# Up to layer 0's first scores: the adaLN scale into 128 columns, gates in program order, V's weights split beside them, an order by hand for K, Q and V

## The chip, the cores and the metric

One Trainium2 chip, one of its cores. The time is the device time of one launch in microseconds (us). For the kernel before the median of three runs is given, and one further execution was recorded by the hardware profiler; the rows quoted come from that one. Engines go by the profile's names: PE (TensorE), DVE (VectorE), ACT (ScalarE), POOL (GpSimd) and SP, whose queue issues most transfers.

## What is computed

Two layers over 1024 latent tokens and 256 context tokens of 1024 features. Layer 0 is multi-head latent attention with 16 heads. All that the change touches lies in layer 0, up to the first scores:

```python
m = jax.nn.silu(cvec) @ w + b            # adaLN: shift, scale, gate of each sample
shift, scale, gate = jnp.split(m, 3, axis=-1)
h = x * (1.0 + scale[:, None, :]) + shift[:, None, :]
h_c = ctx * (1.0 + scale_c) + shift_c
q_lat, kv_lat, k_pe, gate = jnp.split(t @ w_in, splits, axis=-1)   # 256, 128, 32 and 1024 columns
q = (rms_norm(q_lat, g_qa) @ w_qb).reshape(bsz, n, A_HEADS, A_NOPE + A_ROPE)
kv = (rms_norm(kv_lat, g_kva) @ w_kvb).reshape(bsz, n, A_HEADS, A_NOPE + A_V)
```

Then come rotary terms on the 32-column parts, attention over all 1280 keys, o times silu(gate), a product with out_w and a layer norm. The context's modulation vector is c_ctx, the latents' is c.

## The kernel before

Tokens lie in ten tiles of 128: 0 to 7 are latents, 8 and 9 the context. A float32 product is three products of a high and a low half (`mm3`, L184 to L187): high by high, low by high, high by low; a split is a rounded copy on ACT (L176) and a subtraction (L177) on DVE or POOL.

**Start (L205 to L264).** The eight row blocks of adaLN's scale weights (`g` = 1) and shift weights (`g` = 0) arrive in a ring of six buffers `adaw`. For the scale PE forms two rows of 1024 (one for each sample, products L229 of 512 columns); they are copied out by ACT, turned into columns by eight small transposes (`rows_to_cols`, L192) and copied to `cols0` by DVE. For the shift DVE sums the weights into `hacc` (L233), and PE reduces over the partitions by eight products with one column of ones (L243), first for sample 1 (context), then for sample 0; DVE copies these (L244). Then `h_part` scales and shifts x: ACT the high half hH (L254), DVE the full value (L255), DVE or, for every third block, POOL the low half hL (L257). Context comes first, then tokens 0 to 511, then the rest beside the latent tiles.

**Latents (L338 to L368).** For tiles 8, 9, 0, 1 and on, PE makes 416 columns of latents (24 products), ACT and POOL the norms, DVE `ln` (L363); two tiles later `lat_post` turns ln (L331) and splits it into latH and latL. Then the first two gate tiles follow.

**Gates (L310, L520 to L546).** Four blocks of 256 gate columns by ten tiles, 24 products each, into bank tags a and d; ACT applies silu and stores. Beside each gate tile two steps of the generator `side` run: `up_weights` (weights of Q and K scaled on DVE, split on ACT and POOL; rotary part of K; squares on ACT L425 to L429 whose column sums PE takes, L414; scale factors) and `ada_dve` (three thirds of adaLN's weights summed over the blocks on DVE, L467 and L469; PE reduces over the partitions, L476, or for the last third L488). Behind them `ab1_of` and `h1_range` (L505 to L518) make the factors of layer 1. In this stage the order on every engine is the scheduler's; ahead of it, in the latents, and after it PE follows the program (`manual_schedule`).

**K, Q, V (L573 to L826).** V's weights are loaded, scaled by DVE (L291) and split; then K's first pair of heads, Q's rotary part with its rotation, Q's first heads and V's ten tiles, each product into one of three pairs of banks `a`, which ACT empties (high half, L181 or L592) and then DVE (low half, L182 or L598; for odd V tiles ACT L595 and POOL L596). `max0` (L682) takes each row's largest score: four products and reductions (L695), a last one for the context keys (L700), and a product that puts the bound into Q (L704, L705). The first scores of attention are L769.

**Attention.** `run_step` (L736) interleaves the scores' units of one head with side work for the next ones, in program order on PE.

## Time and profile before

| what | us |
|---|---|
| median of three runs (lowest to highest) | 1840.31 (1835.49 to 1841.04) |
| the profiled execution's own time | 1831.31 |
| its span | 1829.5 |
| PE busy in the span | 1680.2 (92%) |
| DVE, ACT, POOL busy | 1238.1, 1104.9, 812.0 |
| first gate product at | 96.12 |
| gates until | 240.3 |
| first scores (L769) at | 276.34 |

A row of the windows gives a stretch of the span, its length, the busy time of each engine with its number of instructions, the clock that PE was granted (1.00 is full), the share of time that the transfer engines were busy and what they moved. A row of the timeline gives start, length, engine, line, operation, what it writes and reads, and in brackets how long the engine was idle ahead of it and what ended that. A group's row gives a count, busy time, mean of one in ns and idle time ahead. PE's records overlap: a product's record is longer than its distance to the next.

### The profile page before, as it was taken

To read this page: it belongs to the slowest core of one execution; us is meant where nothing else is said; L and a number is where in the kernel's file an instruction comes from. 1 tells how busy PE (TensorE), PEld (TensorE's weight loads), DVE (VectorE), ACT (ScalarE), POOL (GpSimd) and SP (SyncE) were. 2 spreads that over 40 slices of the span, in tenths; PEclk is the share of its full clock that TensorE was granted. 3 is DMA by queue.
4 is the path that set the end of the run, shared out by engine and by line. 5 is a ranking of instruction groups with operands and counts; after the bars stand their busy time and mean duration, and the time that the engine had idled before them with its cause. 6 is when DMAs were issued, how large, how long until landed. Compare 5 with 4: busy or idle time off the path is not lost. (4 is left out here: it accounts for less than half of the span.)

```text
span 1829.5 us, 36574 instructions
## 1 busy us (share of the span) xinstructions
PE 1680.2 (92%) x14468; PEld 1229.2 (67%) x14468; DVE 1238.1 (68%) x2054; ACT 1104.9 (60%) x2223; POOL 812.0 (44%) x719
## 2 busy tenths in 40 slices
PE   7899989999999998979999999999899999886998
PEld 3889965666666655567766666767575767575776
DVE  7546765565565666636754877787777787879674
ACT  3442157877877777825435576757676676757442
POOL 1443026767767776737551323231313131435454
PEclk9999999999999999999999999999999999999999
DMA  8246630111110122164432213121212122223331
GB/s 305 71 127 191 192 109 18 40 33 37 40 45 23 40 56 68 55 211 150 142 109 76 77 53 78 53 74 52 60 41 63 44 58 62 66 60 110 100 124 70
DMA packets 111225, 154.84 MB, mean 85 GB/s; under 512 B 13415, under 2 KB 84679, under 8 KB 111054
## 3 DMA queue, kind: packets, MB, share of 16 engines
q1 hardware_dynamic: 102654, 144.90, 26.7%
q10 hardware_dynamic: 8400, 7.61, 1.3%
q8 instruction: 114, 1.87, 0.4%
q14 instruction: 57, 0.47, 0.1%
HBM read 98.65 MB, written 27.07 MB: 69 GB/s over the span
## 5 line engine op out<-in xcount | busy, mean ns | idle before, releaser
L715 POOL TENSOR_TENSOR pl<-p,ph 128x1024 f16<-128x1024 f32 (+1 forms) x176 | 364.2, 2075 | 148.0 <-ACT ph L714 121.6
L1259 ACT ACTIVATE p<-ps_b,mx 128x512 f32<-128x512 f32 (+1 forms) x384 | 230.7, 618 | 85.5 <-DVE mx L1255 81.3
L713 ACT ACTIVATE p<-ps_a,esc 128x1024 f32<-128x1024 f32 (+1 forms) x176 | 189.2, 1075 | 94.4 <-PE ps_a L771 86.9
L695 DVE TENSOR_REDUCE mx<-ps_a 128x1 f32<-128x1024 f32 x128 | 155.5, 1222 | 134.0 <-PE ps_a L693 134.0
L714 ACT CAST ph<-p 128x1024 f16<-128x1024 f32 (+1 forms) x176 | 177.1, 1006 | 5.5
L1253 DVE TENSOR_REDUCE mx<-ps_b 128x1 f32<-128x512 f32 x256 | 165.3, 679 | 0.0
L784 PE MATMUL ps_d<-Vh,pl 128*128 128x65 f16 x1344 | 145.9, 194 | 3.9 <-POOL pl L715 3.9
L781 PE MATMUL ps_d<-Vh,ph 128*128 128x65 f16 x1344 | 148.0, 195 | 0.0
L783 PE MATMUL ps_d<-Vl,ph 128*128 128x64 f16 x1344 | 146.8, 193 | 0.0
L1236 PE MATMUL ps_b<-KS,QS 128*128 128x512 f16 (+1 forms) x384 | 126.9, 347 | 12.7 <-DVE pl L182 6.9
L1284 POOL TENSOR_TENSOR sm<-sm,us 128x1 f32<-128x1 f32 x64 | 17.1, 267 | 272.2 <-DVE sm L1263 268.7
L781 PEld LDWEIGHTS <-ph 128*128 128x128 f16 x1344 | 123.2, 97 | 18.0 <-issue 4.8
L783 PEld LDWEIGHTS <-ph 128*128 128x128 f16 x1344 | 123.9, 98 | 12.0
L1237 PE MATMUL ps_b<-KS,Q 128*128 128x512 f16 (+1 forms) x384 | 129.8, 347 | 0.0
L769 PE MATMUL ps_a<-qH,KH 100*128 100x512 f16 x320 | 122.0, 381 | 7.7 <-ACT p L713 3.8
L784 PEld LDWEIGHTS <-pl 128*128 128x128 f16 x1344 | 123.1, 97 | 5.3 <-POOL pl L715 5.3
L1272 PE MATMUL ps_b<-idr,p 128*128 128x128 f32 x640 | 103.1, 277 | 25.4 <-ACT p L1259 16.8
L182 DVE SCALAR_TENSOR_TENSOR pl<-ps_b,lcf,ph 128x512 f16<-128x512 f32 (+1 forms) x192 | 117.2, 653 | 13.4 <-ACT ph L181 13.4
L181 ACT ACTIVATE ph<-ps_b,lcf 128x512 f16<-128x512 f32 (+1 forms) x192 | 115.3, 648 | 17.8 <-PE ps_b L1272 17.8
L770 PE MATMUL ps_a<-qH,KL 96*128 96x512 f16 x320 | 121.8, 381 | 0.0
L771 PE MATMUL ps_a<-qL,KH 96*128 96x512 f16 x320 | 121.2, 379 | 0.0
L1282 PE MATMUL ps_b<-vh,pl 128*128 128x128 f16 x640 | 111.3, 220 | 5.3 <-DVE pl L182 5.3
(412 smaller groups left out, 5270.3 us busy)
## 6 DMA issues: line engine op xcount, KB each, us to landing
ws<-in_dw SPq DMA_DIRECT2D x28, 512.0 KB, 3.9
adw<-in_ada_w SPq DMA_DIRECT2D x24, 512.0 KB, 4.6
adaw<-in_ada_w SPq DMA_DIRECT2D x16, 512.0 KB, 5.9
g<-sg_d SPq DMA_DIRECT2D x16, 512.0 KB, 3.6
sg_d<-gg ACTq DMA_DIRECT2D x40, 128.0 KB, 2.9
o_d<-op SPq DMA_DIRECT2D x7, 640.0 KB, 3.7
xt<-in_xT SPq DMA_DIRECT2D x16, 256.0 KB, 3.5
wgs<-in_w_in SPq DMA_DIRECT2D x32, 128.0 KB, 2.3
```

Source lines behind the costliest of these rows:

```text
L695: dve.tensor_reduce(mx[:, t, 0:1], ps, axis=AX.X, op=ALU.max)
L713: act.activation(p32[:, :n], st, AF.Exp, scale=esc0)
L714: act.copy(ph[:, :n], p32[:, :n])
L715: pool.tensor_tensor(pl[:, :n], p32[:, :n], ph[:, :n], op=ALU.subtract)
L769: pe.matmul(s_, kh[:nr, ks], QH[:nr, :], start=True, stop=False)
L781: pe.matmul(pv[:, t, :], ph[:, ts], Vh[:, k, h, :], start=(k == kcs[0] and t == 0), stop=False, skip_group_check=True)
L783: pe.matmul(pv[:, t, :V0], ph[:, ts], Vl[:, k, h, :], start=False, stop=False, skip_group_check=True)
L784: pe.matmul(pv[:, t, :], pl[:, ts], Vh[:, k, h, :], start=False, stop=(k == NT - 1), skip_group_check=True)
L1236: pe.matmul(out, qs[m][:, ts], ks[m][:, c0:c0 + n], start=True, stop=False)
L1237: pe.matmul(out, q1[m][:, ts], ks[m][:, c0:c0 + n], start=False, stop=True)
L1253: dve.tensor_reduce(mx[:, 2 + 2 * m + i:3 + 2 * m + i], b, axis=AX.X, op=ALU.max, negate=True)
L1259: act.activation(p[m][:, c0:c0 + n], b, AF.Exp, bias=nb, accum_out=sm[:, 2 + 3 * m + i:3 + 3 * m + i])
```

## The change

- **Scale.** POOL copies silu(c) to 128 columns (`scb`, the two samples in turn); PE multiplies each 128-column piece of the weights by it, so that the sums stand in PSUM as columns; two DVE additions bring them to `cols0`. The row with adaLN's bias takes one of the six `adaw` slots. PE follows the program from here until K, Q and V.
- **Shift.** PE multiplies by all 128 columns of ones. The context's comes first; four products with an identity and the first half of tile 8 follow, then the other sample's, then the rest of tile 8.
- **Latents.** `lat_post` runs three tiles behind, with one more buffer for ss, rs and ln.
- **Gates.** One step of `side` for each gate tile. `up_weights` works in a ring of five buffers `u`, its low halves are DVE's, squares are summed one square later. `ada_dve` has three buffers acc; a third's column sums stand beside the next third's additions. V's weights are split beside the last block of gates.
- **Layer 1's range** (`h1_range`) runs within the first step of attention, in parts.
- **K, Q, V.** PE and DVE follow an order by hand: Q's rotary part first, then K, then V's first tile, Q, and on. Even V tiles go by ACT and POOL, odd ones by DVE.

The diff, cut to its core:

```diff
+    rowb = hs.tile([P, D], F32, tag="adaw", bufs=6, name="rowb")[0:1, :]
...
-    bks = [bank("a"), bank("a")]
-    for j in range(2):
-        pe.matmul(bks[j][:2, :], ones[0:1, 0:2], rowb[:, j * 512:(j + 1) * 512], start=True, stop=False)
+    man = ExitStack()
+    man.enter_context(tc.manual_schedule(engines={ENG[c] for c in MAN}))
+    cbs = [bank("c").rearrange("p (j n) -> p j n", j=4) for _ in range(2)]
+    scb = hs.tile([P, KT, P], F32, name="scb")
+    pool.tensor_copy(scb.rearrange("p k (n s) -> p k n s", s=2),
+                     sc.rearrange("p (k o s) -> p k o s", o=1, s=2).to_broadcast([P, KT, 64, 2]))
+    for j in range(KT):
+        pe.matmul(cbs[j // 4][:, j % 4, :], rowb[:, j * P:(j + 1) * P], ones[0:1, :], start=(j % 4 == 0), stop=False,
+                  skip_group_check=True)
...
             if g:
-                for j in range(2):
-                    pe.matmul(bks[j][:2, :], sc[:, 2 * k:2 * k + 2], w[:, j * 512:(j + 1) * 512],
-                              start=False, stop=(k == KT - 1))
+                for j in range(KT):
+                    pe.matmul(cbs[j // 4][:, j % 4, :], w[:, j * P:(j + 1) * P], scb[:, k, :], start=False,
+                              stop=(k == KT - 1), skip_group_check=True)
...
-    for j in range(2):
-        act.copy(rows[:, j * 512:(j + 1) * 512], bks[j][:2, :])
-    rows_to_cols(rows, cols0, "c", 8, 8)
-    dve.tensor_scalar_add(cols0[:, 8:16, :], cols0[:, 8:16, :], 1.0)
-    for s in (1, 0):
-        cb = bank("b")
+    for i in range(2):
+        dve.tensor_scalar_add(cols0[:, 8 + 4 * i:12 + 4 * i, :], cbs[i][:, :, 0:2], 1.0)
+
+    def shift_cols(s):
+        cb = bank("d")
         for j in range(KT):
-            pe.matmul(cb[:, j:j + 1], acc[s][:, j * P:(j + 1) * P], ones[:, 0:1], start=True, stop=True)
-        dve.tensor_copy(cols0[:, 0:8, s], cb[:, :8])
+            pe.matmul(cb[:, 32 * j:32 * j + P], acc[s][:, j * P:(j + 1) * P], ones, start=True, stop=True)
+        with tc.high_priority():
+            dve.tensor_copy(cols0[:, 0:8, s], cb[:, :256].rearrange("p (j n) -> p j n", j=KT)[:, :, 0])
+
+    def lat_mm(ps, t, ks):
+        ts = slice(t * P, (t + 1) * P)
+        for k in ks:
+            mm3(ps[:, :NA], hH[:, k, ts], hL[:, k, ts], wAH[:, k, :], wAL[:, k, :], k == 0, k == KT - 1)
+
+    shift_cols(1)
     for k in (6, 7):
...
-    for i in (2, 0):
-        for k in range(KT):
-            h_part(hs, 14, *CHUNKS[i], k)
+    for k in range(KT):
+        h_part(hs, 14, *CHUNKS[2], k)
+    ps8 = bank("a")
+    for _ in range(4):
+        pe.matmul(ps8[:, :NA], idr, wAH[:, 0, :], start=True, stop=True)
+    lat_mm(ps8, 8, range(4))
+    shift_cols(0)
+    for k in range(KT):
+        h_part(hs, 14, *CHUNKS[0], k)
+    lat_mm(ps8, 8, range(4, KT))
...
+    def kv_weight(c, hi, lo, ws, e_lo=pool):
...
 
         hk = iter(range(KT))
         todo = []
-        for t in (8, 9, 0, 1, 2, 3, 4, 5, 6, 7, None, None):
-            if len(todo) == 2 or t is None:
+        for t in (8, 9, 0, 1, 2, 3, 4, 5, 6, 7, None, None, None):
+            if len(todo) == 3 or t is None:
                 lat_post(*todo.pop(0))
                 next(gw, None)
...
-            ts = slice(t * P, (t + 1) * P)
-            ps = bank("a" if t % 2 == 0 else "b")
-            for k in range(KT):
-                mm3(ps[:, :NA], hH[:, k, ts], hL[:, k, ts], wAH[:, k, :], wAL[:, k, :], k == 0, k == KT - 1)
+            ps = ps8
+            if t != 8:
+                ps = bank("a" if t % 2 == 0 else "b")
+                lat_mm(ps, t, range(KT))
...
                 rstd_of(rs, ss, 1.0, 2)
-                ln = pa.tile([P, NA], F32, tag="ln", bufs=3, name=nm("ln"))
...
+        u = lambda w=768: pa.tile([P, 768], F32, tag="u", bufs=5, name=nm("u"))[:, :w]
...
+        def q_weight(j, hh):
+            c = slice(hh * 768, hh * 768 + 768)
+            ws = u()
+            sp.dma_start(ws, w_qb[j * P:(j + 1) * P, c])
+            dve.tensor_scalar_mul(ws, ws, gqa[:, j:j + 1])
+            split(wqH[:, j, c], wqL[:, j, c], ws)
...
+        def k_weight(hh):
             c = slice(hh * 512, hh * 512 + 512)
-            kv_weight(c, wkH[:, c], wkL[:, c], rot(pa, [P, 512], F32, "wkv"))
...
+        def column_sums(sq, i, c0, first, stop):
+            if first:
+                cur[0] = bank("c")
+            pe.matmul(cur[0], onr, sq, start=first, stop=stop)
...
+            kt = u(512)[:ROPE]
             sp.dma_start(kt[:, :n], kp_d[:, c])
             if c0 < SEQ:
-                tabs = []
+                tabs = [u(512)[:ROPE] for _ in range(2)]
...
+        def square(f, i, c0, first, stop):
+            sq = u(512).bitcast(F32R) if i else pa.tile([P, 512], F32R, tag="wsq", bufs=2, name=nm("wsq"))
+            f(sq, slice(c0, c0 + 512))
+            wait.append((sq, i, c0, first, stop))
+            if len(wait) == 2:
+                column_sums(*wait.pop(0))
+
+        sq = [(square, a) for a in jobs]
+        rc = [(rope_chunk, a) for a in CHUNKS]
+        for f, a in ([(q_weight, (j, hh)) for j in range(2) for hh in range(2)] + [(k_weight, (hh,)) for hh in range(2)]
+                     + sq[:2] + rc + sq[2:]):
+            f(*a)
             yield
-
...
+        end = iter(())
+
+        def add(k, s):
+            ck = sc[:, 2 * k + s:2 * k + s + 1]
+            if k == 0:
+                acc.append(tile_("acc"))
+                dve.tensor_scalar_mul(acc[s], ws[k], ck)
+            else:
+                dve.scalar_tensor_tensor(acc[s], ws[k], ck, acc[s], op0=ALU.mult, op1=ALU.add)
+
+        for layer, g in thirds:
+            acc, ws = [], []
+            for k in range(KT):
+                ws.append(tile_("adw"))
+                sp.dma_start(ws[k], ada_w[layer, k * P:(k + 1) * P, g * D:(g + 1) * D])
+                if k == 0:
+                    continue
+                if k == 1:
+                    add(0, 0)
+                    add(1, 0)
+                    yield
+                    next(end, None)
+                    add(0, 1)
+                    add(1, 1)
+                    yield
+                else:
+                    next(end, None)
+                    add(k, 0)
+                    add(k, 1)
+                    yield
+            end = finish(layer, g, acc)
+        for _ in end:
+            yield
 
...
+    def h1_range(bank_):
 
         for i in range(2):
             dve.tensor_reduce(hm[:, i:i + 1], ab1[:, i, :, :].rearrange("p a b -> p (a b)"), axis=AX.X, op=ALU.max,
                               apply_absolute_value=True)
+        yield
+        bk = bank_()
...
-            yield from up_weights(sp_)
+            for i, _ in enumerate(up_weights(sp_)):
+                if i in (1, 3, 5, 7, 9, 13, 17):
+                    yield
...
+            t_ = lambda tag: sp_.tile([P, D], F32, tag=tag, bufs=3, name=nm(tag))
+            yield
+            yield
+            yield from ada_dve(t_, ((1, 0), (1, 1), (0, 2)))
+
+    def v_weight():
+        with spool("vwst", side="right") as vs:
+            for hh in range(2):
+                c = slice(hh * 512, hh * 512 + 512)
+                kv_weight(slice(1024 + hh * 512, 1536 + hh * 512), wv[0][:, c], wv[1][:, c],
+                          vs.tile([P, 512], F32, tag="wvs", bufs=2, name=nm("wvs")))
+                yield
...
+            else:
+                pgr_ctx.close()
+                vwp = rp.enter_context(spool("vw", side="right"))
+                wv = [vwp.tile([P, 1024], F32R, name=n_) for n_ in ("wvH", "wvL")]
+                gw = v_weight()
             while gcount[q] < NT:
                 gate_tile(q, wH, wL)
                 if gcount[q] > 1:
                     next(gw, None)
-                for _ in range(2):
-                    next(side, None)
-        for _ in side:
+                next(side, None)
+        for _ in chain(gw, side):
             pass
-    ab1_of()
-    h1_range(bank("c"))
     p0.close()
...
-            if t % 2:
+            if t % 2 == 0:
...
             src = proj_pair(slice(cw, cw + P), WQ2, QS2, p0_, pn)
             if p0_ < SEQ:
-                src = rope(src, pn, cosA, sinA, w0("rsw"), w0("rr"))
-            split16(sH[:, p0_:p0_ + pn], sL[:, p0_:p0_ + pn], src, qsc0)
-            yield
+                sw, r = w0("rsw"), w0("rr")
+                yield from rope(src, pn, cosA, sinA, sw, r, 1 - h)
+                src = r[:, :pn]
+            pH, pL = sH, sL
+            if h:
+                split16(pH[:, p0_:p0_ + pn], pL[:, p0_:p0_ + pn], src, qsc0)
+                yield
...
             ps = proj_pair(slice(h * NOPE, h * NOPE + P), WQ2, QS2, p0_, pn)
             split16(sH[:, p0_:p0_ + pn], sL[:, p0_:p0_ + pn], ps, qsc0)
+            yield
+        if h == 0 and b != 1:
+            split16(pH[:, p0_:p0_ + pn], pL[:, p0_:p0_ + pn], src, qsc0)
             yield
...
     man.close()
+    pk, pq, pq1, pq2 = prod_k(0), prod_q(0, 0), prod_q(0, 1), prod_q(0, 2)
+    pm = max0(0, 0)
+    with tc.manual_schedule(engines={ET.PE, ET.DVE}):
+        for g in (pq, pk, pq, vg, pq, pq, vg, pk, pk, pq, pq1, vg, pq2, pq2, pq2, vg,
+                  pm, vg, pm, vg, pm, vg, pm, vg, pm, vg, pm, vg):
+            next(g)
...
+            if h == 0:
+                ab1_of()
+            hr = [(h1_range(pair), (0, 1, 0, 1, 1))] if h == 0 else []
+            run_step(units0(h, 0), hr + [(max0(h, 1), (1, 1, 2, 1, 1)), (max0(h, 2), (0, 1, 0, 1)),
```

How instructions move, at three places. First PE at the start: before, from the last scale products on (ps_a here are the two rows, hacc the shift's sums, ps_a_381 tile 8).

```order
L229 MATMUL ps_a_137<-adaw_219,sc 2x512
L229 MATMUL ps_a_138<-adaw_219,sc 2x512
L192 MATMUL ps_c_233<-idr,rows 128x2 x8
L243 MATMUL ps_b_244<-ones,hacc_133 128x1 x8
L243 MATMUL ps_b_254<-ones,hacc_132 128x1 x8
L185 MATMUL ps_a_381<-wAH,hH 128x416
```

The same place in the change (ps_a_351 is tile 8; the twelve products of its first half are cut to the first and last three).

```order
L228 MATMUL ps_c_141<-scb,adaw_273 128x128 x4
L228 MATMUL ps_c_142<-scb,adaw_273 128x128 x4
L241 MATMUL ps_d_293<-ones,hacc_135 128x128 x8
L269 MATMUL ps_a_351<-wAH,idr 128x416 x4
L185 MATMUL ps_a_351<-wAH,hH 128x416
...
L185 MATMUL ps_a_351<-wAH,hH 128x416
L186 MATMUL ps_a_351<-wAL,hH 128x416
L187 MATMUL ps_a_351<-wAH,hL 128x416
L241 MATMUL ps_d_368<-ones,hacc_134 128x128 x8
L185 MATMUL ps_a_351<-wAH,hH 128x416
```

The transposes are gone, and the second shift stands inside tile 8. Second, PE among the gates: before, the sum of one square between two gate tiles (wsq is a square, wgH and wgL gate weights).

```order
L187 MATMUL ps_a_1240<-wgH_374,hL 128x256
L414 MATMUL ps_c_1272<-wsq_1197,onr 128x512
L185 MATMUL ps_d_1278<-wgH_374,hH 128x256
L186 MATMUL ps_d_1278<-wgL_375,hH 128x256
L187 MATMUL ps_d_1278<-wgH_374,hL 128x256
```

In the change, three of them at one such joint (u is the ring of five).

```order
L187 MATMUL ps_a_1283<-wgH_452,hL 128x256
L418 MATMUL ps_c_1320<-wsq_1222,onr 128x512
L418 MATMUL ps_c_1326<-u_1318,onr 128x512
L418 MATMUL ps_c_1331<-u_1324,onr 128x512
L185 MATMUL ps_d_1335<-wgH_452,hH 128x256
```

Sums that stood a tile apart now stand in one group, and the next gate tile behind it. Third, DVE in the K/Q/V stage: before, from V's weights on (p is V's weights, stk, stq and stp the halves of K, Q and Q's rotary part, rsw and rr the rotation).

```order
L516 TENSOR_SCALAR hic<-kci 128x1
L291 TENSOR_SCALAR p_337_2506<-p_337_2506,gkva 128x512
L182 SCALAR_TENSOR_TENSOR stkL_2494<-ps_a_2524,ksc_69,stkH_2493 128x1024
L291 TENSOR_SCALAR p_337_2506<-p_337_2506,gkva 128x512
L182 SCALAR_TENSOR_TENSOR stkL_2494<-ps_a_2533,ksc_69,stkH_2493 128x256
L277 STREAM_SHUFFLE rsw_2491<-ps_a_2541 128x1024
L278 TENSOR_TENSOR rr_2492<-ps_a_2541,cs_2500 128x1024
L279 TENSOR_TENSOR rsw_2491<-rsw_2491,cs_2504 128x1024
L182 SCALAR_TENSOR_TENSOR stqL_2496<-ps_a_2560,qsc_70,stqH_2495 128x1024
```

In the change:

```order
L499 TENSOR_TENSOR acc_2159<-adw_2411,ps_c_2451 1x512
L290 STREAM_SHUFFLE rsw_2536<-ps_a_2562 128x1024
L291 TENSOR_TENSOR rr_2537<-ps_a_2562,cs_2545 128x1024
L182 SCALAR_TENSOR_TENSOR stkL_2539<-ps_a_2577,ksc_69,stkH_2538 128x1024
L294 TENSOR_TENSOR rsw_2536<-rsw_2536,cs_2549 128x1024
L295 TENSOR_TENSOR rr_2537<-rr_2537,rsw_2536 128x1024
L182 SCALAR_TENSOR_TENSOR stqL_2541<-ps_a_2599,qsc_70,stqH_2540 128x1024
L182 SCALAR_TENSOR_TENSOR stpL_2543<-rr_2537,qsc_70,stpH_2542 128x1024
L656 SCALAR_TENSOR_TENSOR Vl<-ps_a_2616,vsc_68,Vh 128x1024
```

V's weights and the range are gone from here, and the rotation leads. From the first scores on, the rows of every engine follow in the same order in both kernels, but for the range's, which the change has in the first step of attention.

155 lines of the change are left out of this document (54 added, 101 removed).

## The prediction

> **What bounds the kernel now.** I read the share of busy time first, then the windows cut at the joints of the part that changes (start, latents, gates, K/Q/V), then the waits of PE in each joint, then the timeline where the windows showed holes. From the first scores at 276.3 us on, each engine has the same instructions in the same order but for one small piece, so what is won or lost ahead of that point goes straight to the end. The windows' columns: start and end, length, busy us of PE, PEld, DVE, ACT, POOL, granted clock, DMA share, GB/s.
>
> ```profile
> 4.00:30.00 26.00, 19.77 (x36) 2.59 (x34) 20.32 (x20) 3.32 (x7) 0.00 (x0) 1.00 1.00 382
> 30.00:36.00 6.00, 6.00 (x50) 5.97 (x49) 3.97 (x6) 3.50 (x8) 2.67 (x2) 0.92 1.05 335
> 36.00:42.00 6.00, 5.85 (x17) 4.97 (x17) 5.85 (x16) 6.00 (x11) 1.68 (x2) 0.51 0.63 200
> ...
> 48.20:51.70 3.50, 0.05 (x2) 0.02 (x1) 3.50 (x9) 0.84 (x4) 3.16 (x5) 1.00 0.07 25
> 51.70:55.40 3.70, 3.70 (x13) 3.42 (x14) 3.40 (x8) 3.42 (x9) 0.39 (x2) 0.55 0.00 0
> ...
> 70.70:95.90 25.20, 25.19 (x142) 24.55 (x143) 7.85 (x19) 8.61 (x37) 4.45 (x10) 1.00 0.02 5
> ...
> 96.00:240.30 144.30, 137.05 (x1054) 132.05 (x1053) 86.36 (x116) 35.93 (x89) 36.65 (x37) 0.95 0.60 175
> 240.30:276.30 36.00, 28.70 (x123) 20.49 (x121) 27.08 (x40) 23.32 (x26) 14.10 (x9) 0.95 0.29 83
> ```
>
> Up to 30 us the transfers are full (share 1.00), so the weights' arrival sets the pace there, and the change moves the same bytes. From 30 us on PE sets it: busy or waited for throughout, DVE beside it only at 36 to 51 us. PE loses time in two ways, idle stretches and the half clock behind them (0.51 and 0.55 above). The waits name the idle ones (us in all, times, longest):
>
> ```profile
> PE ps_c L331 <- DVE ln L363: 5.7, 2, 3.5
> PE ps_c L476 <- DVE acc L469: 3.0, 1, 3.0
> PE ps_c L414 <- ACT wsq L425: 2.6, 1, 2.6
> PE ps_c L414 <- ACT wsq L428: 1.6, 1, 1.6
> PE ps_a L185 <- DVE Vl L598: 2.7, 2, 2.1
> ...
> ```
>
> The first four stand in the latents and the gates, in program places that the change rewrites; the last is the longest of the K/Q/V stage.
>
> **Term 1: start and latents.** Timeline rows of the start (start us, length, engine, line, operation):
>
> ```profile
> 25.05 1.88 PE L229 MATMUL ps_a<-adaw,sc 128*2 128x512 f32 x4 [1.28 <-DMA adaw<-in_ada_w]
> 28.21 1.88 PE L229 MATMUL ps_a<-adaw,sc 128*2 128x512 f32 x4 [1.28 <-DMA adaw<-in_ada_w]
> 29.55 2.48 DVE L233 SCALAR_TENSOR_TENSOR hacc<-adaw,sc,hacc 128x1024 f32<-128x1024 f32 x2 [0.18 <-DMA adaw<-in_ada_w]
> 31.89 4.19 PE L243 MATMUL ps_b<-ones,hacc 128*128 128x1 f32 x32
> 36.11 0.17 DVE L244 COPY cols<-ps_b 128x8 f32<-128x8 f32 x1 [1.75 <-PE ps_b L243]
> 36.20 0.42 DVE L255 TENSOR_SCALAR xt<-xt,cols 128x256 f32<-128x256 f32 x1
> 49.76 1.28 DVE L257 TENSOR_TENSOR hL<-xt,hH 128x512 fp32r<-128x512 f32 x2
> 51.69 0.67 PE L331 MATMUL ps_c<-idr,ln 128*128 128x128 f32 x3 [3.45 <-DVE ln L363]
> 58.33 0.49 PE L331 MATMUL ps_c<-idr,ln 128*128 128x128 f32 x3
> 96.12 0.37 PE L185 MATMUL ps_a<-wgH,hH 128*128 128x256 f32 x1
> L331 PE MATMUL ps_c<-idr,ln 128*128 128x128 f32 x27 | 4.7, 282 | 5.7 <-DVE ln L363 5.7
> ```
>
> The scale's two products of 512 columns (four records, 1.88 us a tile of weights) become eight of 128 columns, sixteen records if each makes two as before. Their size isn't in the trace: L243's records, which load 128x128 weights as these must but move one column, take 4.19/32 = 0.131; those of L331, with 128 columns, 4.7/27 = 0.174. So 2.1 to 2.8 us for each tile of weights, and both fit the tiles' period of 3.16 (28.21 less 25.05): nothing piles up, and the last ends at 30.3 to 31.0. The copies, eight transposes and the row-to-column copy go. The context's shift (sixteen records as well, 2.1 to 2.8) can begin when DVE has summed that half, 29.55 + 1.24 = 30.8, so DVE has all columns of the context at 33.1 to 33.9, and I take its first x-part at 33.7 (bounds 33.1 and, should the wide records be twice as dear, 37) against 36.20: 2.5 us earlier. The other sample's shift now stands inside tile 8, where PE waits for DVE's parts anyway.
>
> From there DVE paces the first three tiles: 36.20 to 49.76 + 1.28 = 51.04 is 14.8 us, so now to 48.5, and PE can end tile 0 some 0.9 us later (three products and what it is behind), 49.4, where it ended at 58.33. That works because the change runs tile 0 ahead of the first transposes: the wait for ln (3.45 us) has tile 0's 24 products in its place. What is late next is ln itself: L363 stands behind the x-parts on DVE, so ln comes at about 48.7, and PE, which ends tile 0 at 49.4, finds it there. The second hole (5.7 less 3.45, 2.3 us, one tile later) had the same lag of two tiles; with three I leave 0.7 us for it. The seven tiles and posts behind it took 96.12 - 58.33 = 37.8, less that 2.3: 35.5. So the latents end at 49.4 + 0.7 + 35.5 = 85.6, **-10.5 us**. Half of it is idle time (5.7 less 0.7), the rest is the half clock at 36 to 42 and 51.7 to 55.4 (0.49 x 6.0 and 0.45 x 3.7 make 4.6 us at most) and the earlier start. Four idle-filling products of 416 columns keep PE active ahead of tile 8; should the clock stay at half through tile 8 nevertheless, DVE paces that stretch and it costs little. Bounds: -5 (columns at 37, one hole left) and -12.
>
> The Trainium skill's "TensorE: Matmul & The Clock Gate" (Part 1: The HAM clock gate) says that a quiet window of about 3.4 us halves the clock and a busy one of that length restores it. The rows agree: the 2.3 us hole left 1.00 behind it (70.70 to 95.90), that of 3.45 was followed by 0.55. By that rule the four fillers, which are shorter than the window, need not keep the clock up alone; were tile 8 to begin cold, an estimate from the page's figure is 3.4 x 0.5 = 1.7 us, which lies inside the bounds.
>
> **Term 2: gates.** Forty gate tiles, and beside them the up-weights, three sums over adaLN weights, and their columns.
>
> ```profile
> 151.99 0.28 PE L185 MATMUL ps_a<-wgH,hH 128*128 128x256 f32 x1
> 154.87 0.28 PE L185 MATMUL ps_d<-wgH,hH 128*128 128x256 f32 x1
> 130.14 0.41 PE L186 MATMUL ps_d<-wgL,hH 128*128 128x256 f32 x1
> 130.35 0.38 PE L187 MATMUL ps_d<-wgH,hL 128*128 128x256 f32 x1
> 123.30:132.30 9.00, 4.87 (x25) 4.56 (x25) 4.57 (x9) 3.41 (x7) 2.59 (x2) 0.81 0.25 75
> 188.00:190.00 2.00, 2.00 (x12) 2.00 (x11) 2.00 (x3) 0.00 (x1) 0.00 (x0) 0.50 0.63 115
> L507 PE MATMUL ps_c<-idr,hm 128*128 128x128 f32 x4 | 0.6, 273 | 0.0
> L469 DVE SCALAR_TENSOR_TENSOR acc<-adw,sc,acc 128x1024 f32<-128x1024 f32 x42 | 54.2, 1358 | 2.5 <-DMA adw<-in_ada_w 2.5
> L177 POOL TENSOR_TENSOR wgL<-wgs,wgH 128x256 fp32r<-128x256 f32 x24 | 22.5, 961 | 24.2 <-ACT wgH L176 24.2
> ```
>
> A warm tile takes 154.87 - 151.99 = 2.88. At half clock a product takes 0.21 (130.35 less 130.14) in place of 0.12. Idle in the stage: 144.30 - 137.05 = 7.25. Half clock: behind the 2.6 us hole 0.19 x 9.00, 1.7 at most, of which I take 1.5; behind the 3.0 hole 10 us from 182 to 192, five windows of 2 us like the one shown. At 0.12 for 0.21 these are 4.3 lost at most; I take 3.5, since column sums, which move one column, lie among them. L507 leaves (0.6). Together 12.85 us that could go. The change gives each thing a distance, in steps of one gate tile: a square is summed only when the next has been issued, a third's columns are taken one step behind its last additions, and three acc buffers let DVE begin the next third before. But PE now takes all in program order: behind a column sum that isn't ready stand all gate tiles. The critical place is the same, the first column sums of a third, one step (2.88) behind its last two additions (2 x 1.36 = 2.7): just in time. So I leave 3 us for waits and their half clock (bounds 0 and all 12.85): **-9.9 us**. The six low halves that move from POOL to DVE should take what its subtraction takes, 0.64 for 512 columns (1.28 for two, L257) and so 0.96 for 768: 5 us of DVE's 58 idle ones here (144.30 less 86.36), at no cost unless DVE falls behind (third rival). V's weights (two loads on SP's queue, two scalings L291, two high halves on ACT, two low ones on POOL) go beside the last ten tiles, 29 us in which nothing but a third's additions stands on DVE; the loads wait only for the last gate weights to be through the queue.
>
> Where POOL reads at the same time, DVE's two-input operations stretch: 0.66 alone, 1.73 beside a split.
>
> ```profile
> 111.56 1.73 DVE L278 TENSOR_TENSOR kr<-kt,ktab 32x512 f32<-32x512 f32 x1
> 120.45 0.66 DVE L278 TENSOR_TENSOR kr<-kt,ktab 32x512 f32<-32x512 f32 x1
> ```
>
> The Trainium skill's "SBUF — State Buffer" (SBUF: two separate sides) calls the pair of ports that DVE and POOL share an exclusive lock, held for a whole instruction. It speaks against moving the low halves to DVE; by it each could wait for one gate-weight split, 6 x 0.96 = 5.8 us of DVE at worst, which is inside DVE's idle time, so the sum stays.
>
> **Term 3: K/Q/V.** Here PE idles 7.3 us of 36.0: three pairs of banks, each drained by ACT and then DVE.
>
> ```profile
> L592 ACT ACTIVATE Vh<-ps_a,vsc 128x1024 f16<-128x1024 f32 x10 | 11.2, 1117 | 5.8 <-PE ps_a L187 5.7
> L598 DVE SCALAR_TENSOR_TENSOR Vl<-ps_a,vsc,Vh 128x1024 f16<-128x1024 f32 x5 | 6.4, 1276 | 2.1 <-ACT Vh L592 2.1
> L291 DVE TENSOR_SCALAR p<-p,gkva 128x512 f32<-128x512 f32 x2 | 1.8, 876 | 0.0
> 240.79 0.42 DVE L508 TENSOR_REDUCE hm<-ps_c 128x2 f32<-128x256 f32 x1 [8.47 <-PE ps_c L507]
> 242.88 0.14 DVE L516 TENSOR_SCALAR hic<-kci 128x1 f32<-128x1 f32 x1
> ```
>
> DVE is freed of 1.8 (V's weights) and of the range's chain, 240.79 to 243.02 = 2.2 us, at the very head; the order puts the rotary part first, whose DVE chain is longest, and V tiles between. Drains still pair ACT and DVE, so not all idle time goes: **-3 us**, bounds 0 and -7.3.
>
> **Term 4: the range moved.** Its 2.2 us of small DVE operations, its 0.6 of PE and one pair of banks now stand in the first attention step, ahead of DVE operations that PE soon waits for. **+1.5** (bounds 0 and 2.8).
>
> **Sum.** -10.5 - 9.9 - 3 + 1.5 = -21.9. The profiled execution took 1831.3 (span 1829.5 and 1.8 around it), so 1809.4; it lies 9.0 under the median of the three runs shown (1840.3), so in their terms **1818.4 us**, -1.2%. A measurement of this kernel can tell about 0.3%, 5.5 us.
>
> **Rivals.** *The waits come back in the gates* (0.20). Each hole of 3 us is now in program order and moves rather than goes; for it: the first sums of a third are just in time; and ahead of the squares' second batch DVE has two rotary chunks, eight operations of 0.66 to 1.73 by the rows above (5 to 14 us), whose buffers the squares take over, with few tiles of 2.88 as cover. The stage keeps its 12.25: 1818.4 + 9.3 = 1828. Against it: more yields of distance at each place. *The start isn't earlier* (0.15): 128-column products twice as dear (over 3.16 us a tile) pile up, columns come at 37, and DVE paces the tiles from there: the latents win 5, not 10.5: 1824. For it: no row shows this form. *DVE falls behind* (0.10, slower): two additions now go with one gate tile of 2.88 us, so from 1.44 us each on, DVE is late; it has 1.36 in the row above. There is one wgL split (0.96) for two additions: if each met one in full, an addition would be 1.28 + 0.48 = 1.76, 0.64 us late a tile, 15 us over 24 tiles, in three holes of 5 us, each with 3.5 of half clock: 26 in place of 3. The low halves on DVE would be late for the squares as well (the 4.2 us of L414 and its 1.5 stay), and K/Q/V would start behind a late DVE (its 3 lost): 1818.4 + 23 + 5.7 + 3 = 1850. From about 1.7 us for an addition the change is slower. Against it: before, with the same splits on POOL, they cost 1.36.
>
> The forecast has 0.50; the remaining 0.05 is more than expected (all holes gone: 1811). Forecast, first two rivals and the better case make 0.90 of faster; mixtures of their losses take 0.08 of it to within 5.5 us of before. Faster 0.82, same 0.08, slower 0.10. Range: up from 1808 (every term near its better bound, some 10 us) to 1834 (two of the rivals' losses together); the forecast's own is 1812 to 1825.
>
> **What would show it.** First x-part of DVE at 33.7 and the first gate tile at 85 to 87, with no row of clock 0.5 ahead of it; gates of 133 to 136 us with under 4 us of PE idle; first scores 33 us behind them; the first attention step 1 to 2 us longer. I am wrong if the adaLN additions' mean passes 1.44, if the wide scale products cost over 0.2 us a record, or if PE waits for a square or a sum for over 3 us anywhere among the gates.

## The result, and the profile after

| | before | changed |
|---|---|---|
| median of four runs, us | 1838.95 | 1812.21 |
| lowest to highest | 1835.49 to 1841.04 | 1811.31 to 1815.74 |
| ratio, with 95% interval | | 0.986 (0.9839 to 0.9881) |
| profiled execution's span | 1829.5 | 1813.8 |

The change is 26.7 us faster by the medians. The two profiled executions differ by 15.7 only, and the difference of the two is the first thing to understand: where do executions of one kernel part?

The windows of the changed kernel, cut at the same joints (start and end, length, busy PE, PEld, DVE, ACT, POOL, clock, share of transfers, GB/s):

```profile
30.00:37.00 7.00, 6.71 (x36) 6.32 (x35) 5.73 (x8) 1.86 (x4) 3.37 (x2) 0.67 0.89 255
37.00:45.00 8.00, 7.20 (x40) 6.06 (x41) 6.69 (x17) 5.63 (x11) 1.67 (x2) 1.00 0.56 175
...
54.30:89.40 35.10, 35.10 (x199) 34.26 (x198) 19.71 (x37) 19.28 (x68) 16.66 (x25) 1.00 0.24 71
89.40:222.80 133.40, 130.88 (x1056) 125.96 (x1054) 89.77 (x122) 38.11 (x93) 27.46 (x33) 1.00 0.63 190
222.80:258.50 35.70, 28.64 (x121) 20.53 (x120) 23.24 (x22) 21.46 (x23) 12.34 (x7) 0.92 0.31 81
```

The gates (89.4 to 222.8) have 2.5 us of PE idle and the full clock throughout; before it was 7.25 and 0.95. The latents behind 54 us have no hole. The K/Q/V stage is as long as it was, with 7.1 us idle. The waits of PE in the gates and in K/Q/V (us in all, times, longest):

```profile
PE ps_c L418 <- DVE u L294: 1.3, 1, 1.3
PE ps_c L418 <- ACT wsq L407: 1.2, 1, 1.2
```

```profile
PE ps_a L768 <- DVE ng L765: 2.1, 1, 2.1
PE ps_a L185 <- DVE stqL L182: 2.1, 1, 2.1
```

The start is not what the prediction drew. Its timeline on PE and DVE in the changed kernel:

```profile
26.52 2.61 PE L228 MATMUL ps_c<-scb,adaw 128*128 128x128 f32 x16 [2.59 <-DMA adaw<-in_ada_w]
29.69 3.78 PE L228 MATMUL ps_c<-scb,adaw 128*128 128x128 f32 x16 [0.56 <-DMA adaw<-in_ada_w]
33.26 2.69 PE L241 MATMUL ps_d<-ones,hacc 128*128 128x128 f32 x16
```

```profile
31.88 3.29 DVE L232 SCALAR_TENSOR_TENSOR hacc<-adaw,sc,hacc 128x1024 f32<-128x1024 f32 x2
35.09 1.45 DVE L177 TENSOR_TENSOR wAL<-ws,wAH 128x416 fp32r<-128x416 f32 x1
36.47 0.15 DVE L236 TENSOR_SCALAR cols<-ps_c 128x8 f32<-128x8 f32 x1
...
37.36 0.41 DVE L261 TENSOR_SCALAR xt<-xt,cols 128x256 f32<-128x256 f32 x1 [0.67 <-ACT hH L260]
```

The seventh tile of scale weights came at 26.5 (before: 25.05), PE fell to the half clock (0.67 in the window above), the last products took 3.8 us, and the first x-part of DVE came at 37.36, later than the 36.20 of before. And yet the first gate product stands at 89.43 and not at 96.12.

### The profile page after: what moved, and what is told of

The parts are those of the page before. It is cut to its first block, busy times and chain, and to the rows that moved or that the text cites. A ratio compares the mean times of both kernels' runs of the same rounds, so it can differ in the third digit from the quotient of the medians.

```text
span 1813.8 us, 36751 instructions
## 1 busy us (share of the span) xinstructions
PE 1674.7 (92%) x14564; PEld 1242.0 (68%) x14564; DVE 1244.8 (69%) x2057; ACT 1104.4 (61%) x2221; POOL 798.8 (44%) x714
## 5 line engine op out<-in xcount | busy, mean ns | idle before, releaser
L1347 POOL TENSOR_TENSOR sm<-sm,us 128x1 f32<-128x1 f32 x64 | 16.1, 251 | 272.4 <-DVE sm L1326 268.4
```

## The experiments

Stage marks of all profiled executions, in us from each span's start: the first gate product, the first product of K/Q/V, the first scores, and as a last mark the 41st of the 48 bounds that DVE puts into Q (L705, in the change L769), far into attention. From the third of these bounds to the 41st the fourteen profiles take 417.0 to 420.2 us, so that differences at the last mark are what the changed part won or lost, to about 3 us; behind it executions of these kernels differ by up to 7 us (1118.2 to 1125.3 us to the end), and I saw no cause for that in the edits.

| kernel | first gate | K/Q/V | first scores | last mark | median of its runs |
|---|---|---|---|---|---|
| before, first profile | 96.12 | 240.5 | 276.3 | 707.4 | |
| before, second profile (`r_before`) | 97.96 | 248.4 | 284.6 | 716.9 | 1835.0 to 1839.0 in the four sets |
| changed, first profile | 89.43 | 222.8 | 258.5 | 692.0 | 1812.21 |
| changed, second (`r_after`) | 87.92 | 221.7 | 255.7 | 688.5 | 1812.43 |
| `x_start_old` | 91.10 | 226.8 | 260.7 | 693.4 | 1818.67 |
| `x_lag2` | 96.09 | 241.6 | 277.2 | 712.3 | 1831.78 |
| `x_lag2_cover` | 97.74 | 234.5 | 268.4 | 701.1 | 1826.02 |
| `x_before_lag3` | 90.94 | 241.9 | 275.3 | 705.6 | 1830.38 |
| `x_gates_auto` | 88.00 | 220.2 | 254.2 | 686.8 | 1809.06 |
| `x_side_late` | 87.15 | 218.8 | 255.8 | 690.9 | 1813.36 |
| `x_h1_head` | 89.68 | 224.0 | 259.3 | 688.9 | 1809.08 |
| `x_vpar` | 88.01 | 221.5 | 254.9 | 689.9 | 1808.40 |
| `x_tail` | 87.82 | 221.2 | 256.4 | 692.2 | 1811.99 |
| `x_best` | 87.67 | 221.1 | 255.3 | 684.3 | 1805.39 |

### Both kernels once more

No edit.

> The changed kernel once more. In its first profile the latents won 6.7 us, not 10.5: the seventh tile of adaLN's scale weights came 1.5 us later than before (product at 26.52, before 25.05), PE then stood at the half clock from 27 to 34.5 us, and the first x-part came at 37.36, not 33.7. Theory: that is this one execution's transfer delay and the clock it brought; another execution has the product at about 25.1, the clock at 1.00 through 36 us, the first x-part at 34 to 35.5, the first gate tile at 86 to 87.5, and a span 2 to 4 us below 1813.8. Rival: the ring is the cause (one slot goes to the bias row, and PE holds each slot 2.05 us, not 1.88): then every execution shows 26.5, 37.4 and 89.4, and spans differ elsewhere.

> The kernel before once more, for a second profile: its first profiled execution (1831.3) lay 4 to 10 us below its other runs. Theory: the difference between executions lies outside the part that changes, so the first gate product is again at 96, K/Q/V at 240 and the first scores at 276, all within 1 us, and what differs stands behind 276 us. Rival: the start varies by transfers and the half clock, and a slower execution shows these three marks 3 to 8 us later.

The waits of PE in the gates of the second profile of before, and its window:

```profile
PE ps_c L414 <- ACT wsq L428: 5.1, 1, 5.1
PE ps_c L476 <- DVE acc L469: 3.9, 1, 3.9
PE ps_c L414 <- ACT wsq L425: 2.8, 1, 2.8
```

```profile
98.00:248.40 150.40, 138.49 (x1054) 133.45 (x1053) 87.61 (x116) 35.56 (x89) 38.05 (x38) 0.93 0.57 168
```

The three waits that the first profile of before had (1.6, 3.0, 2.6) are 11.8 us here, and the clock is 0.93, not 0.95: the stage takes 150.4 us, not 144.4. My theory for `r_before` (they part behind 276 us) fell; the rival was right as to size, but the place is the gates. The kernel before thus varies in its gates by 6 us; the changed kernel's took 133.4 and 133.8. The mean over both profiles of each kernel is 712.1 at the last mark before and 690.2 after: 21.9 us.

The windows of the changed kernel's second profile:

```profile
30.00:36.00 6.00, 4.76 (x37) 4.22 (x37) 5.22 (x9) 2.37 (x5) 3.10 (x2) 1.00 0.86 261
36.00:42.00 6.00, 5.59 (x32) 4.46 (x33) 5.58 (x15) 3.63 (x8) 1.66 (x2) 1.00 0.86 287
...
54.00:87.90 33.90, 33.90 (x193) 33.20 (x192) 18.69 (x35) 17.97 (x65) 16.42 (x24) 1.00 0.26 74
87.90:221.70 133.80, 130.80 (x1055) 125.89 (x1053) 90.51 (x122) 37.82 (x93) 28.10 (x33) 1.00 0.63 190
221.70:255.70 34.00, 26.51 (x121) 19.14 (x120) 23.24 (x22) 21.39 (x23) 11.67 (x7) 1.00 0.32 86
```

Here the clock stays at 1.00, the first x-part comes at 35.87 and the first gate at 87.92, 1.5 us sooner; so the half clock doesn't come in every execution (of the kernels below with this start, `x_lag2_cover` has 0.64 and `x_h1_head` 0.87 from 30 to 36 us). The late weights do come in every one: the seventh tile was again used at 26.60, after 2.15 us of waiting, and in all ten profiles with the new start it is used at 25.89 to 27.06, in the four with the old start at 24.69 to 25.05. That half of the rival holds. The bias row's slot isn't the cause, since `x_start_old` keeps it and has that tile at 24.82; whether it is PE holding each slot for 2.05 us in place of 1.88 was not separated.

### The start alone

`x_start_old` puts the start of the kernel before into the changed one: rows, eight transposes and a copy for the scale, shifts of one column, both of them ahead of tile 8, and no fillers.

```diff
-                for j in range(KT):
-                    pe.matmul(cbs[j // 4][:, j % 4, :], w[:, j * P:(j + 1) * P], scb[:, k, :], start=False,
-                              stop=(k == KT - 1), skip_group_check=True)
+                for j in range(2):
+                    pe.matmul(bks[j][:2, :], sc[:, 2 * k:2 * k + 2], w[:, j * 512:(j + 1) * 512],
+                              start=False, stop=(k == KT - 1))
...
-            pe.matmul(cb[:, 32 * j:32 * j + P], acc[s][:, j * P:(j + 1) * P], ones, start=True, stop=True)
+            pe.matmul(cb[:, j:j + 1], acc[s][:, j * P:(j + 1) * P], ones[:, 0:1], start=True, stop=True)
...
-    for _ in range(4):
-        pe.matmul(ps8[:, :NA], idr, wAH[:, 0, :], start=True, stop=True)
```

> The change with the start as before (scale as rows, eight transposes, both shifts ahead of tile 8, no filler products); lag of three tiles, gates and K/Q/V as changed. My prediction's theory (columns 2.5 us earlier): this is 2 to 3 us slower than the change. Rival, from the change's first profile (x-parts at 37.36 there, 36.20 before): the start wins nothing by itself, this is as fast as the change or up to 1 us faster, and what the latents won comes from the lag of three tiles: first gate product at 86 to 89.

It is 6.2 us slower by the medians (0.9901, interval 0.9875 to 0.9928, beside 0.987, 0.9847 to 0.9893, of the change on the same chip), and 1.4 to 4.9 at the last mark. Its x-parts came at 37.74, and the clock was half through the first tile:

```profile
30.00:36.00 6.00, 6.00 (x42) 5.98 (x41) 3.49 (x6) 3.25 (x7) 2.66 (x2) 0.73 1.02 329
36.00:42.00 6.00, 5.85 (x20) 5.04 (x21) 4.31 (x13) 6.00 (x12) 1.11 (x2) 0.50 0.49 171
```

So the new start is worth 1.7 to 3.2 us at the first gate (91.10 against 89.43 and 87.92). At this place the size is the one expected by my theory, 2 to 3 us (the medians' 6.2 is more, and the marks don't show where), but not by columns that come early. In `x_start_old` DVE copies the context's columns at 34.24 and in the kernel before at 33.88, sooner than in the change (36.54 and 35.05). There the x-parts stand behind the other sample's copy, for which DVE waits 3.17 and 1.75 us; in the change it stands behind them. So the x-parts of the change come at 35.87 at best, 0.3 us sooner than before.

The half clock of the old start (0.50 above; 1.00 from 36 to 42 us in both profiles of the change) is only a part of the loss. The first transposes, behind tile 0, start at 53.99 in `x_start_old` and at 54.09 and 52.61 in the change. The other 1.8 us are lost behind them, most of them in two waits of PE for late x-parts of tokens 512 and on:

```profile
74.35 0.45 PE L187 MATMUL ps_a<-wAH,hL 128*128 128x416 f32 x1 [1.05 <-DVE hL L262]
75.53 0.46 PE L187 MATMUL ps_a<-wAH,hL 128*128 128x416 f32 x1 [0.35 <-DVE hL L262]
```

Neither profile of the change has a wait there; `x_before_lag3` below, with the same start, has them too (1.04 and 0.34). `x_start_old` takes back the wide products, the place of the second shift and the fillers at once, so which of them does it was not separated.

### The lag of three tiles

```diff
-        for t in (8, 9, 0, 1, 2, 3, 4, 5, 6, 7, None, None, None):
-            if len(todo) == 3 or t is None:
+        for t in (8, 9, 0, 1, 2, 3, 4, 5, 6, 7, None, None):
+            if len(todo) == 2 or t is None:
```

> The change with the transposes two tiles behind, as before, and its own start. Theory: the lag of three tiles is what removes the holes in front of L331; without it the 3.5 us hole and its half clock come back (3.5 + 1.7) and the 2.3 us one, so the first gate product is at 93 to 96 (change 88 to 89.4) and the kernel 5 to 7.5 us slower. Rival: the earlier second shift and the split of tile 8 have moved the norms far enough, the holes come back by half: 1 to 3 us.

19.4 us slower than the change (1831.78; ratio to before 0.9967, 0.9952 to 0.9982): with all else of the change in place, this one number is worth most of the gain. The first gate is back at 96.09, 0.03 us from before, as expected, but the gates are long again as well. The three largest waits of PE from 30 us to the end of the gates, and the window of the gates:

```profile
PE ps_c L346 <- DVE ln L378: 5.9, 2, 4.3
PE ps_c L418 <- ACT wsq L407: 4.2, 1, 4.2
PE ps_c L486 <- DVE acc L511: 3.5, 1, 3.5
```

```profile
96.10:241.60 145.50, 136.87 (x1052) 131.38 (x1050) 89.82 (x121) 36.84 (x91) 28.80 (x33) 0.95 0.59 175
```

Neither of my two theories had this. With a lag of three, three gate tiles stand in the latents' loop, not two, and the steps of side work begin behind them; each column sum so stands one gate tile (2.9 us) further from the latents' end, behind which the loads for it are issued (the first of Q's weights at 105.32 here and 98.62 in `r_after`). The wait on the first square is 4.2 here and 1.6 in `r_after`: the difference is near that one tile. Two kernels test it.

### One tile of cover, given back and given alone

`x_lag2_cover` keeps the lag of two and leaves out one step of the side work at the first gate tile behind the latents:

```diff
-                next(side, None)
+                if q or gcount[q] != 3:
+                    next(side, None)
```

> The change with the lag of two (1831.8, gates 145.5 us, waits of 4.2 on the first square and 3.5 on the first sums) and one step of the side work left out at the first gate tile behind the latents, so that each sum stands one gate tile later, as with a lag of three. Theory (cover): the two waits shrink to about 1.3 and under 1, no half clock behind them, gates at 133 to 137, the kernel 8 to 12 us faster than with the lag of two, first gate product still at 96. Rival (the longer latents with their holes make the side work late in themselves, by transfers queued behind them): gates stay at 142 to 146.

The gates take 136.8 us, 8.7 less than with the lag of two alone; the last mark is 11.2 us earlier, the median 5.8 lower (two sets of runs, each against before: 0.994, 0.992 to 0.9961, and 0.9967). The wait on the first sums is gone, that on the first square is 1.5, and one of 2.6 at a later sum of squares is new:

```profile
PE ps_c L418 <- DVE vm L422: 2.6, 1, 2.6
PE ps_c L418 <- ACT wsq L407: 1.5, 1, 1.5
PE ps_c L498 <- DVE acc L511: 0.6, 1, 0.6
```

```profile
97.70:234.50 136.80, 132.19 (x1051) 126.98 (x1050) 88.07 (x121) 36.95 (x91) 30.00 (x33) 0.99 0.62 186
```

The cover theory holds for the changed side work, by its waits and by the stage. The medians' 5.8 us fall short of the 8 to 12 that it expected; the profiled execution of `x_lag2` (1834.17) was among the slower of its ten. `x_before_lag3` gives the same lag to the kernel before:

```diff
-        for t in (8, 9, 0, 1, 2, 3, 4, 5, 6, 7, None, None):
-            if len(todo) == 2 or t is None:
+        for t in (8, 9, 0, 1, 2, 3, 4, 5, 6, 7, None, None, None):
+            if len(todo) == 3 or t is None:
-                ss = pa.tile([P, 2], F32, tag="ss", bufs=2, name=nm("ss"))
+                ss = pa.tile([P, 2], F32, tag="ss", bufs=3, name=nm("ss"))
-                rs = pa.tile([P, 2], F32, tag="rs", bufs=2, name=nm("rs"))
+                rs = pa.tile([P, 2], F32, tag="rs", bufs=3, name=nm("rs"))
-                ln = pa.tile([P, NA], F32, tag="ln", bufs=3, name=nm("ln"))
+                ln = pa.tile([P, NA], F32, tag="ln", bufs=4, name=nm("ln"))
```

> The kernel before with one edit: the transposes stand three tiles behind (and one more buffer for ss, rs and ln), so that three gate tiles stand in the latents, not two. Lag of two in the change gave the gates their old 145.5 us. Theory (cover): side work's weights come a fixed time behind the latents, and each gate tile that stands ahead of the first sum is 2.9 us of cover for every later joint: here too the latents win 5 to 6 us and the gates 6 to 12, the kernel is 11 to 18 us faster than before. Rival (the side work's new distances do it, the lag only the latents): 4 to 7 us faster, gates at 143 to 151 as before.

7.5 us faster than before (0.9956, 0.9939 to 0.9974): the rival, just above its upper bound. The latents win their 5 to 7 us (first gate at 90.94), and the gates keep everything:

```profile
PE ps_c L476 <- DVE acc L469: 4.3, 1, 4.3
PE ps_c L414 <- ACT wsq L428: 2.9, 1, 2.9
PE ps_c L414 <- ACT wsq L425: 1.3, 1, 1.3
```

```profile
90.90:241.90 151.00, 142.55 (x1060) 137.87 (x1057) 85.75 (x117) 36.51 (x92) 35.55 (x38) 0.91 0.56 163
```

So the gates' 11 to 17 us come from two edits together, and neither shows a gain there alone: the side work's new distances (without the third tile: 145.5) and the third tile (without the distances: 151.0), beside 144.4 and 150.4 before. Which of the new distances counts (ring of five, later sums, a third buffer acc, one step for each gate tile, low halves on DVE) was not separated.

### Program order, and one more tile

`x_gates_auto` leaves the order of the gates to the scheduler (the stretch of fixed order is closed ahead of `ada_dve` and opened again behind the gates), `x_side_late` leaves out one side step in the change (the diff above with 4 for 3).

```diff
+    man.close()
...
     p0.close()
+    man.enter_context(tc.manual_schedule(engines={ENG[c] for c in MAN}))
```

> The change with the order in the gates left to the scheduler, as before; the side work as changed (ring of five, sums one square later, three acc buffers, low halves on DVE). The stage took 144.2 and 150.5 us in the two profiles of before, 133.4 and 133.8 in those of the change. Theory A (the distances in the side work do it): the stage takes 133 to 137. Theory B (the fixed order of PE does it, the scheduler puts sums where their inputs are late): it takes 140 to 150, with single waits of over 3 us before L418 or L486 and the half clock behind them. My prediction leant on A and feared the fixed order.

> The change with one step of the side work left out at the first gate tile. Theory (cover): the change's last two waits in the gates, 1.6 and 1.3 us before L418, go as well, the stage is 2 to 3 us shorter, the kernel 1 to 3 us faster than the change. Rival: the later third ends behind the last gate tile, its sums then stand bare ahead of K/Q/V: no gain, or up to 3 us slower.

The order by hand wins nothing: 132.2 us with the scheduler's (1809.06; 0.9853, 0.9833 to 0.9873), 133.4 and 133.8 with the program's. Theory B falls; A holds only together with the third tile, as `x_lag2` shows.

```profile
88.00:220.20 132.20, 130.48 (x1055) 126.00 (x1053) 90.44 (x122) 37.70 (x93) 29.26 (x33) 1.00 0.64 192
```

One more tile of cover makes the stage 131.6, its waits 1.4 in all, and the kernel no faster (1813.36, 0.9873, 0.9852 to 0.9893). The 2 us are lost again in K/Q/V, which took 37.0 us at a clock of 0.92, with a wait of 1.4 for the rotation (`rr L291`) that the change has not:

```profile
87.20:218.80 131.60, 130.15 (x1054) 125.67 (x1053) 90.44 (x122) 37.84 (x93) 28.79 (x33) 1.00 0.63 186
218.80:255.80 37.00, 29.06 (x121) 20.75 (x120) 23.27 (x22) 21.39 (x23) 12.65 (x8) 0.92 0.35 105
```

How much of that is chance isn't settled: of the eight profiles with the change's order in K/Q/V, four show a clock below 1.00 there (0.92 to 0.95) and four 1.00.

### Layer 1's range

```diff
+    ab1_of()
+    for _ in h1_range(lambda: bank("c")):
+        pass
     p0.close()
-            if h == 0:
-                ab1_of()
-            hr = [(h1_range(pair), (0, 1, 0, 1, 1))] if h == 0 else []
+            hr = []
```

> The change with layer 1's range back ahead of K/Q/V, its first place. Theory: in attention's first step its DVE operations make PE wait 1.4 us (L768 behind hm) and cost 1.5 to 2.5 in all, at the head of K/Q/V they cost 0.6 of PE and hide on DVE, which waits 8 us there for its first rotation: this is 1 to 2 us faster than the change. Rival: the place ahead of K/Q/V costs as much, since the matrix product of the range waits for the last sums: no difference, or up to 2 us slower.

3.4 us faster than the change by the medians (1809.08; 0.9853, 0.983 to 0.9877, beside 0.987, 0.9847 to 0.9893); the intervals overlap, and the last mark (688.9) lies between the change's two. Counted from the first gate, which the edit doesn't touch, the last mark comes 1.3 to 3.3 us sooner than in the change. The profiles say why. The change's second profile, in attention's first step on DVE, and then PE:

```profile
268.12 1.76 DVE L556 TENSOR_TENSOR hm<-hm 128x1 f32<-128x1 f32 x1
269.80 0.14 DVE L557 SCALAR_TENSOR_TENSOR hm<-hm 128x1 f32<-128x1 f32 x1
...
271.35 0.74 DVE L769 SCALAR_TENSOR_TENSOR qH<-ps_a,sh,selt 4x512 f16<-4x512 f32 x1
```

```profile
270.17 0.22 PE L768 MATMUL ps_a<-idr,ng 128*4 128x128 f32 x1 [1.44 <-DVE hm L300]
272.14 0.38 PE L833 MATMUL ps_a<-qH,KH 100*128 100x512 f16 x1 [1.38 <-DVE qH L769]
```

PE waits 1.44 + 1.38 = 2.8 us, and that is what the marks lose from the first of these bounds to the third (from 21.1 to 18.3 us ahead of before's first profile). In `x_h1_head` the same operation takes 0.16, and PE waits 0.5 at the joint:

```profile
224.18 0.16 DVE L556 TENSOR_TENSOR hm<-hm 128x1 f32<-128x1 f32 x1
```

### K, Q and V: parity and the tail

`x_vpar`, with V's odd tiles on ACT and POOL as before, and `x_tail`, with L764 ahead of the ninth V tile:

```diff
-            if t % 2 == 0:
+            if t % 2:
```

```diff
-                  pm, vg, pm, vg, pm, vg, pm, vg, pm, vg, pm, vg):
+                  pm, vg, pm, vg, pm, vg, pm, pm, vg, vg, pm, vg):
```

> The change with V's odd tiles on ACT and POOL and the even ones on DVE, as before. In the change the rotation's last addition on DVE (L295) takes 3.06 us instead of 1.21, beside POOL's subtraction of V's first tile, and PE then waits 2.1 us for stqL. Theory: L295 is back at 1.21, the wait shrinks to under 0.5, and the stage of 34.0 us (at full clock) is 1 to 2 us shorter. Rival: V's first low half, 1.28 us, now stands in DVE's chain itself, POOL meets the next operation: no change within 0.7 us, or longer.

> The change with one edit in the order by hand: the last reduction over the context's keys (L764) stands ahead of the ninth V tile, not behind it. In the change DVE idles 1.76 us for that tile's high half with L764's input ready, and PE then waits 2.1 us for ng, which is followed by the half clock in one profile of two. Theory: the wait goes, the stage is 1.5 to 2 us shorter and the half clock at its end does not come. Rival: the V tile's banks are then freed later and PE waits there instead: under 0.5 us.

In the change the rotation's last addition runs beside POOL's first V subtraction, in `x_vpar` alone. The rows of the change on DVE and on POOL, then of `x_vpar`:

```profile
230.74 3.06 DVE L295 TENSOR_TENSOR rr<-rr,rsw 128x1024 f32<-128x1024 f32 x1
```

```profile
230.65 2.08 POOL L654 TENSOR_TENSOR Vl<-op,Vh 128x1024 f16<-128x1024 f32 x1 [5.59 <-ACT op L653]
```

```profile
229.42 1.22 DVE L295 TENSOR_TENSOR rr<-rr,rsw 128x1024 f32<-128x1024 f32 x1
```

The addition loses 1.84 us and the wait for stqL falls from 2.1 to 0.6, as expected, but the stage takes 33.4 us beside 34.0: the V tile's low half (1.28) now stands in DVE's chain. The median is 1808.40 (0.9845, 0.9824 to 0.9867) beside the change's 1812.2 to 1812.4, but the last mark (689.9) lies between the change's two (688.5 and 692.0), so a gain isn't shown. `x_tail` removes the wait for ng, gets one of 1.1 for Vl and is no faster (1811.99; 0.9862, 0.9842 to 0.9882), as its rival had it. But its stage ran at a clock of 0.90, so what the edit is worth at the full clock isn't shown.

### Four edits together

V's parity, the range ahead of K/Q/V, the scheduler's order in the gates, one side step left out; the diffs are those above.

> Four edits on the change at once: V's parity as before (won 1.1 us in the stage by 34.0 to 33.4 and the wait for stqL), layer 1's range ahead of K/Q/V (1809.1), the gates' order left to the scheduler (1809.1), one side step left out. If they add up: 1812.4 - 3.3 - 3.3 - 1 - 2 = 1802 to 1804. Rival: they compete for the same few us at the joint of gates and K/Q/V: 1806 to 1809.

1805.39 (0.9832, 0.9813 to 0.9851): between the sum and the rival, 7 us under the change by medians of different sets and 4.2 to 7.7 at the last mark. It beats both kernels: its four runs (up to 1808.9) lie under all eight of the change (from 1809.6).

## Why the prediction was right

The forecast was 21.9 us in the profiled execution's terms and 1818.4 for the median; the median is 1812.2, inside the range, and at the very edge of the forecast's own, 1812 to 1825. The four terms, by the two profiles of each kernel:

| term | predicted | measured | from |
|---|---|---|---|
| start and latents | -10.5 | -6.7 to -10.0 | 96.12, 97.96 to 89.43, 87.92 |
| gates | -9.9 | -10.6 to -17.1 | 144.4, 150.4 to 133.4, 133.8 |
| K/Q/V | -3 | -0.1 to -2.2 | 35.8, 36.2 to 35.7, 34.0 |
| the range moved | +1.5 | +1.1 to +3.1 | what is lost from the first scores to the third bound |
| sum | -21.9 | -21.9 | mean at the last mark, 712.1 to 690.2; attention behind the third bound wins 0.6 |

That the two sums are equal is luck. By the means of the two profiles, start and latents won 2.1 us less than I had, K/Q/V 1.8 less, and the range cost 0.6 more; the gates won 3.9 more, and attention the rest. Against the first profile of before alone, from which I forecast, the two profiles of the change are 15.4 and 18.9 us ahead at the last mark.

- **What bounds the kernel** held: what is won ahead of the first scores goes to the end. It is seen in the marks, which from the third bound to the last keep their distance to 0.7 us (14.7 and 15.4 in the first profiles), and over all the profiles to 3.2.
- **The offset of 9.0 us was misread.** I took the profiled execution of before to be 9.0 us short in all its parts alike and added that to the changed kernel. The second profile shows that 6.0 of the 9.5 us between the two lie in the gates, and these are the waits that the change takes away. The longer executions of before had more to win. Of the 6.2 us by which the median beat the forecast, 2.7 are the base: the 33 runs of before in the four sets have a median of 1837.6, not 1840.3. That the rest are these waits fits, but two profiles don't show it. The rows for it were in the prediction, three waits of 1.6 to 3.0 us, and I gave them no spread; the one of 1.6, then 5.1, stands behind a load of Q's weights, for which DVE idles 3.40 us in the first profile and 5.44 in the second.
- **Start: the step that failed.** "DVE has all columns of the context at 33.1 to 33.9": they came at 36.7 and 35.2. The products cost what I bounded (2.05 us a tile of weights, at full clock), so the late columns of the second rival came, but not from its cause. The last two tiles of weights come 1.5 us later than before, the sums hacc with them; on DVE a weight split of 1.45 (L177), which my sum left out, stands ahead of the columns, and behind them the x-part waits 0.67 for ACT's high half. That DVE then paces the tiles, 14.8 us for the first three, is near as a time (tile 0's parts end at 53.44 in the first profile, 16.1 behind the first) but not as a cause: from the second half of tile 8 on, at 42.67 there, PE waits for nothing until the gates.
- **Latents: right by the lag.** That tile 0 replaces the first hole and a lag of three the second is shown by `x_lag2` (5.9 us of waits for ln back, the first gate at 96.09) and `x_before_lag3` (90.94). I left 0.7 us for the second hole; there was none. (In the kernel before it stands at 70.71, three tiles behind the first and not one, as I wrote.)
- **Gates: right in size, incomplete in cause.** I put the gain on the distances in the side work. `x_lag2` has all of them and 145.5 us. The third gate tile in the latents was in the diff and I counted it only as cover for ln. The fixed order that I feared costs 1.2 to 1.6 us at most (`x_gates_auto`). The waits left are 2.5 to 3.0 us, for which I had 3: 1.3 behind the rotary chunks, which the first rival named, and the rest at the first square.
- **DVE did not fall behind.** The additions of the third rival cost 1.35 on average (1.36 in `r_after`), under its point of 1.44:

```profile
L511 DVE SCALAR_TENSOR_TENSOR acc<-adw,sc,acc 128x1024 f32<-128x1024 f32 x42 | 54.2, 1347 | 5.2 <-DMA adw<-in_ada_w 5.0
L177 DVE TENSOR_TENSOR wqL<-u,wqH 128x768 fp32r<-128x768 f32 x4 | 3.8, 950 | 0.0
```

  The moved low halves take 0.95, the estimate was 0.96; that a lock with POOL would stretch them does not show in this row. No kernel was run with them back on POOL.
- **K/Q/V: over-estimated.** The stage's idle time is 7.1 and 7.5 us beside 7.3. What left DVE (V's weights, the range) left it ahead of its first rotation, where it now waits 8 us for PE, so nothing behind it moved; and the new parity put POOL beside the longest chain.
- **The range: right in kind.** The 2.2 us of small operations became 2.8 us of waits in `r_after`, because one of them met a POOL subtraction.

## What to carry to other kernels

Here the joints of the gates were late by their distance from the loads that feed them, not by the order of the engine that waits: count the tiles that stand between the point where the loads can be issued and the first user, and look for an edit elsewhere that changes this count by one. Two edits that each win nothing can win 11 us together, so undo them one at a time before giving either the credit. And take a second profile of the kernel before, since a wait that hangs on transfers has a spread that one profile hides.
